# Input and convolution panels first; memory keys and values after them, with the convolution taps beside; memory queries as a pair

## The chip, the cores and the metric

The kernel runs on one core of a Trainium2 chip. TensorE (PE) multiplies matrices and writes PSUM, eight banks of 128x512 fp32; PEld is its weight loader. VectorE (DVE) and ScalarE (ACT) do elementwise work, GpSimd (POOL) a little, and SyncE (SP) issues the DMAs that bring everything in from HBM. Each engine takes its instructions in a fixed order and they wait for each other by semaphores. The metric is the device time of one execution in microseconds (us): 1532.37 us before, the median of three runs (1531.84 to 1532.49).

## The reference

One decoder layer over x (256 tokens, 4096 features), all in fp32, with 256 memory tokens:

```python
proj = x @ w_in[l]                       # 4096 x 11280
(c_a, c_b, c_gate, g_q, g_k, g_v, g_lr, g_gate, m_q, m_gate) = jnp.split(proj, split_idx, axis=-1)
y_conv = _conv_group(c_a, c_b, ...) * jax.nn.silu(c_gate)
y_gla = _gla_group(g_q, g_k, g_v, g_lr, ...) * jax.nn.silu(g_gate)
y_mem = _memory_group(m_q, mem @ w_mem_kv[l]) * jax.nn.silu(m_gate)
mixed = jnp.concatenate([y_conv, y_gla, y_mem], axis=-1)
out = mixed @ w_out[l]
x = _layernorm(DN_ALPHA * x + out, ln_g[l], ln_b[l])
```

The convolution group takes c_a * sigmoid(c_b), 1024 channels, through a causal depthwise convolution of 31 taps, then a layer norm over the channels and a SiLU. The memory group is attention in four heads of m_q against keys and values that come from mem @ w_mem_kv (4096 x 2048).

## The kernel before, in words

**Split products.** Every fp32 operand is split in two, hi (a rounded copy, made by ACT) and lo (the rest, made by DVE): `halves`, lines 104 and 105. A product is three matmuls: hi-hi, hi-lo, lo-hi. So each 128x1024 piece of weights costs ACT one cast, DVE one subtraction and PE twelve matmuls of 512 columns. Pieces of weights have four hi and four lo buffers (`WBUFS`), raw weights three, and the program writes each piece's making three pieces ahead of its use (`AHEAD`).

**Panels and pairs.** A panel (`panel`, line 342) is 512 columns of w_in for all 4096 features: 16 pieces, 192 matmuls. A pair (`pair`, line 411) does two panels at once in 16 chunks of 1 MB. A chunk written "8" has two pieces and 24 matmuls. A chunk written "7" is a Strassen-like one with 21 matmuls: DVE forms two weight combinations from the raw chunk (`tx`, `ty`, lines 466 to 475) and four pieces are split instead of two, one of them half as wide. It also needs sums of x of the same sort (`sums`, line 157). The table `BY7` holds each pair's pattern of 8s and 7s and the units of x that the 7s use.

**Order before.** Seven warm-up matmuls; then the memory keys and values (`mk`, `mv`: 32 steps of two 512 KB halves, line 222), with mem's and x's eight units loaded on the way (`X_AT`); then the panels in the order of `STEPS`: two pairs for the convolution (cb, ca), two single panels of memory queries (mq), two of q, the pair k, five v, the pairs gg, gg and cg, two mg; then the output projection (three pairs, two panels) and the layer norm.

**The convolution.** A pair's outputs leave PSUM in `pair_done` (line 1022); c_a * sigmoid(c_b) is transposed in 32x32 blocks by DVE and put in place by 16 small copies (line 283, half by ACT and half by DVE). Then come 124 taps for each of the two halves of the channels, 248 in all, each one DVE instruction on 128x226 to 128x256 (lines 852 and 861). They are put in the list `fill`, from which a fixed number per piece (`FILLS`) is written beside the matmuls.

**What sets the order.** The order in which instructions are written is not the final one: the build's scheduler (`schedule_with_timeline_sim=True`, line 1424) puts each engine's instructions in an order of its own, within the dependencies.

Of the kernel before, what the change touches and what calls it, by code (L numbers as in the profile page):

```python
# [27 lines left out]
WARM = 7  # L28
EARLY = 5
AHEAD = 3  # L30
X_AT = (9, 12, 15, 18, 21, 24, 27, 30)

C_A, C_B, C_G, G_Q, G_K, G_V, G_LR, G_G, M_Q, M_G = 0, 1024, 2048, 3072, 4096, 5120, 7168, 7184, 9232, 10256


STEPS = (
    [[("cb", i, [(C_B + 512 * i, 512)]), ("ca", i, [(C_A + 512 * i, 512)])] for i in range(2)]
    + [[("mq", i, [(M_Q + 512 * i, 512)])] for i in range(2)]
    + [[("q", i, [(G_Q + 512 * i, 512)])] for i in range(2)]
    + [[("k", i, [(G_K + 512 * i, 512)]) for i in range(2)]]  # L40
    + [[("v", 0, [(G_LR, 16), (G_V, 400)])]]
# [5 lines left out]


BY7 = {
    ("cb", 0): ("8888878787878787", (0, 1, 2), (), (2,)),  # L50
    ("cb", 1): ("8887888788878887", (0, 1), (), (0, 1)),
    ("k", 0): ("8887888788878887", (0, 1), (0, 1), (0, 1)),
    ("gg", 0): ("8888888788878787", (0, 1), (0, 1), ()),
    ("gg", 2): ("8887888788878887", (0, 1), (), (1,)),
    ("cg", 0): ("8888888788888887", (0,), (), (0,)),
}

FILLS = {("cb", 1): 2, ("mq", 0): 2, ("mq", 1): 3, ("q", 0): 2, ("q", 1): 3}


@with_exitstack
def layer_kernel(ctx, tc, xT, memT, xres, w_mem, w_in, w_pairs, w_last, cst, w_gate,
# [116 lines left out]
    def four(ap):  # L179
        return ap.rearrange("p (k t) -> p k t", k=4)  # L180

    x_units = []
    extX = {}
    m_units = []
    mem_banks = [acc.tile([P, 512], F32, tag="acc", name=f"mk_{i}") for i in range(4)] + [
        bank("mv") for _ in range(4)
    ]

    idle = nc.const_aps.tensor(1.0, [P, 512], BF16)
    for _ in range(WARM):  # L190
        nc.tensor.matmul(mem_banks[7], lhsT=idle[:, 0:P], rhs=idle, start=True, stop=True)
    for kt in range(KT):
        if kt == 0:
            mt0 = unit_tiles("mem")
            m_units.append(load(mt0, four(memT[0]), 0, 1))
        elif kt % 4 == 0:
            m_units.append(load_unit("mem", four(memT[kt // 4])))
        mh, ml = m_units[kt // 4]
        raw = w_raw([P, 2, 1024], "wm")
        for half in range(2):  # L200
            if kt:
                nc.sync.dma_start(
                    out=raw[:, half, :], in_=w_mem[kt][:, 1024 * half : 1024 * half + 1024]
                )
            wt = (raw[:, half, :], *w_tiles([P, 1024], "wm"))
            step = 256 if kt == 0 and half == 0 else 512
            if kt == 0:
                for a in range(0, 1024, step):
                    hi, lo = load(wt, w_mem[kt][:, 1024 * half : 1024 * half + 1024], a, a + step)
                if half == 1:  # L210
                    load(mt0, four(memT[0]), 1, 2)
            else:
                hi, lo = wt[1:]
                halves(*wt)
                if kt == 1 and half == 0:
                    load(mt0, four(memT[0]), 2, 4)
                    give(mt0[0])
            for w, stats in ((hi, (mh, ml)), (lo, (mh,))):
                for a in range(0, 1024, step):
                    for mt in range(2):  # L220
                        for s in stats:
                            nc.tensor.matmul(  # L222
                                mem_banks[half * 4 + a // 512 * 2 + mt][:, a % 512 : a % 512 + step],
                                lhsT=s[:, kt % 4, mt * P : (mt + 1) * P],
                                rhs=w[:, a : a + step],
                                start=kt == 0 and w is hi and s is mh and a % 512 == 0,
                                stop=kt == KT - 1 and w is lo,
                            )
        if kt % 4 == 3:
            give(mh, ml)  # L230
            if kt == 3:
                consts = make_consts(nc, cpool, cst, norm_g)
        if kt in X_AT:
            x_units.append(load_unit("x", four(xT[len(x_units)])))
            if len(x_units) <= 3:
                extX[len(x_units) - 1] = sums(*x_units[-1])
# [11 lines left out]
    mk = [unit([P, 2, 512], F32, "mk") for _ in range(2)]  # L248
    mvh = [unit([P, 2, 512], F32R, "mvh") for _ in range(2)]
    mvl = [unit([P, 2, 512], F32R, "mvl") for _ in range(2)]  # L250
    for nb in range(2):
        for mt in range(2):
            evac(mem_banks[nb * 2 + mt], mk[nb][:, mt, :], mt)
    for nb in range(2):
        for mt in range(2):
            halves(mem_banks[4 + nb * 2 + mt], mvh[nb][:, mt, :], mvl[nb][:, mt, :])

    def queue_transpose(src, dst, then, back=False):  # L260


        st = {}

        def blocks():
            t = tmp.tile([P, 1024], F32, tag="T", name=f"T_{serial[0]}", bufs=1)
            serial[0] += 1
            nc.vector.transpose(out=t, in_=src.rearrange("p a b -> p (a b)"))
            give(src)
            st["t"] = t  # L270
# [34 lines left out]
        queue_transpose(src, scratch, go)  # L305

    mkT = {}
    for i in range(2):
        queue_halves(mk[i], lambda hi, lo, i=i: mkT.update({i: (hi, lo)}))

    def products(ps, terms):

# [98 lines left out]
    def pair(chunks, order, stat, ext, then, soon=KT // 2, fills=0, units=False):  # L411


        banks = {}
# [13 lines left out]
        def summed(j):  # L428
# [2 lines left out]
        a11, a21, a12, a22 = (plain(k, tt) for k in range(2) for tt in range(2))  # L431

        eight = (
            ("b", ((1, a21, "N"), (0, a22, "N"), (1, a11, "3"), (0, a12, "3"))),
            ("a", ((0, a21, "4"), (1, a22, "4"), (0, a11, "2"), (1, a12, "2"))),
        )
        seven = (
# [15 lines left out]
        def make(n, i):  # L453
            c, by7, tiles = plan[n]
            if i == 0:
                raw = w_raw([P, 4, 512], "w")
                nc.sync.dma_start(out=raw, in_=chunks[c].rearrange("p (k n) -> p k n", k=4))
                src = st[n] = dict(a=raw[:, 0:2, :], b=raw[:, 2:4, :], c=raw[:, 2:3, :])
                if by7:
                    serial[0] += 1  # L460
# [27 lines left out]
        def use(n, i):  # L488
# [533 lines left out]
    def pair_done(step, b):  # L1022
# [28 lines left out]

        later.extend((one, two, three, four))

    off = 0
    for step in STEPS:
        width = sum(n for _, _, ranges in step for _, n in ranges)
        size = KT * P * width
        flat = w_in[off : off + size]
# [12 lines left out]
        else:  # L1071
            pattern, by7, fresh, _ = BY7[key]

            def queue_sums(fresh=fresh):
# [10 lines left out]
                soon=6 if key == ("gg", 0) else KT // 2,  # L1085
                fills=fills,
                units=True,
            )

    def give_x():  # L1090
        for hi, lo in x_units:
            give(hi, lo)
        assert not fill

# [252 lines left out]
def make_consts(nc, cpool, cst, norm_g):  # L1347
    ident = cpool.tile([P, P], F32, tag="ident", name="ident")
    make_identity(nc, ident)
    negh = cpool.tile([P, 2], F32, tag="negh", name="negh")  # L1350
    nc.gpsimd.memset(negh, -0.5)
    resetm = cpool.tile([P, 256], F32, tag="resetm", name="resetm")
    nc.gpsimd.memset(resetm, 1.0)
    nc.gpsimd.memset(resetm[:, 0:256:64], 0.0)
    cst_sb = cpool.tile([P, 264], F32, tag="cst", name="cst_sb")
    nc.sync.dma_start(out=cst_sb, in_=cst)
    ng_sb = cpool.tile([P, 512], F32, tag="ng", name="ng_sb")
    nc.sync.dma_start(out=ng_sb, in_=norm_g.partition_broadcast(P))
    return ident, negh, resetm, cst_sb, ng_sb


def lay_out(inputs):
# [73 lines left out]
```

## Time and profile before

| | |
|---|---|
| median of three runs | 1532.37 us |
| the profiled execution | 1533.42 us, span 1531.4 us |
| PE busy | 98%, 6857 matmuls |
| DVE busy | 79% |
| ACT busy | 53% |
| mean granted TensorE clock | 0.994 |

Busy is time in which an engine has an instruction under way; instructions overlap a little at their ends, so the distance from one start to the next is what an instruction costs in a row of them. The profile's 40 slices of 38 us show DVE at nine tenths and more from the eighth to the sixteenth (268 to 613 us), from the second convolution pair's start to past the last tap.

### The profile page before, as it was taken

How to read it: one execution, taken by the hardware profiler on the slowest of the kernel's cores; microseconds unless marked ns; L12 is line 12 of the kernel's file. 1: busy time of each engine (PE TensorE's matmuls, PEld its weight loads, DVE VectorE, ACT ScalarE, POOL GpSimd, SP SyncE). 2: the span in 40 equal slices, each digit the busy share in tenths (PEclk: the TensorE clock that was granted, in tenths of full speed). 3: DMA queues.
4: the chain of work that ended last, by engine and by line, in shares of the span. 5: the costliest groups of instructions: out<-in, count | busy, mean ns of one | idle time of the engine just before them, and what ended most of it. 6: DMA issues, size and time to landing. Idle time of an engine off the chain costs nothing.

```text
span 1531.4 us, 18461 instructions
## 1 busy us (share of the span) xinstructions
PE 1507.0 (98%) x6857; PEld 1271.2 (83%) x6857; DVE 1211.7 (79%) x1567; ACT 819.0 (53%) x1005; POOL 48.0 (3%) x59
## 2 busy tenths in 40 slices
PE   8999999999999999999999999999999999999997
PEld 6888888877888878999999888888888887888885
DVE  7755588999999999867475579796777589898955
ACT  6544565544565556656464456574665454545441
POOL 0000000000000000003030000000000000000001
PEclk9999999999999999999999999999999999999998
DMA  9865546545555546554545555555567645555652
GB/s 352 289 207 195 195 174 220 192 165 196 190 178 180 191 155 232 189 198 159 175 164 183 192 192 190 221 192 205 191 235 258 218 167 212 214 206 208 224 220 110
DMA packets 53650, 307.53 MB, mean 201 GB/s; under 512 B 6004, under 2 KB 6900, under 8 KB 26936
## 3 DMA queue, kind: packets, MB, share of 16 engines
q1 hardware_dynamic: 53560, 306.36, 56.5%
q8 instruction: 53, 0.87, 0.2%
q14 instruction: 37, 0.30, 0.1%
HBM read 302.14 MB, written 4.19 MB: 200 GB/s over the span
## 4 chain that ended last, share of the span: by engine, by line
PE 91%; DVE 5%; DMA 2%; issue 1%; ACT 1%; SPq 0%; POOL 0%; DVEq 0%; ACTq 0%
PE acc L355 34%; PE acc L503 30%; PE acc_N L503 8%; PE sm L503 6%; PE mk L222 5%; PE mv L222 5%; DVE low L105 2%; DVE cacc L861 1%; DMA rawwm<-w_mem 1%; PE o L316 1%; DMA ng_sb<-norm_g 1%; PE A L773 1%; PE sc L316 0%; ACT hiw L104 0%; PE mo L316 0%
## 5 line engine op out<-in xcount | busy, mean ns | idle before, releaser
L104 ACT CAST hiw<-raww 128x1024 fp32r<-128x1024 f32 (+2 forms) x496 | 485.6, 991 | 412.7 <-PE acc L355 203.7
L105 DVE TENSOR_TENSOR low<-raww,hiw 128x1024 fp32r<-128x1024 f32 (+2 forms) x496 | 569.2, 1159 | 146.1 <-ACT hiw L104 128.9
L355 PE MATMUL acc<-hiw,hx 128*128 128x512 f32 (+2 forms) x704 | 261.6, 372 | 1.7 <-ACT ca L1032 1.7
L355 PE MATMUL acc<-hiw,lx 128*128 128x512 f32 (+2 forms) x704 | 261.5, 371 | 0.0
L503 PE MATMUL acc<-hiw,hx 128*128 128x512 f32 x480 | 187.3, 390 | 3.9 <-ACT hiw L104 3.8
L503 PE MATMUL acc<-hiw,lx 128*128 128x512 f32 x480 | 186.9, 389 | 0.0
L355 PE MATMUL acc<-low,hx 128*128 128x512 f32 (+2 forms) x704 | 176.2, 371 | 0.0
L355 PEld LDWEIGHTS acc<-hiw,hx 128*128 128x128 f32 x704 | 132.2, 188 | 17.7 <-ACT ca L1032 2.1
L355 PEld LDWEIGHTS acc<-hiw,lx 128*128 128x128 f32 x704 | 132.2, 188 | 15.4
L355 PEld LDWEIGHTS acc<-low,hx 128*128 128x128 f32 x704 | 130.8, 188 | 15.1
L503 PE MATMUL acc<-low,hx 128*128 128x512 f32 x480 | 140.3, 389 | 0.0
L105 DVE TENSOR_TENSOR lowm<-rawwm,hiwm 128x1024 fp32r<-128x1024 f32 (+2 forms) x68 | 78.7, 1161 | 60.6 <-ACT hiwm L104 60.1
L503 PEld LDWEIGHTS acc<-hiw,hx 128*128 128x128 f32 x480 | 90.1, 188 | 24.4 <-ACT hiw L104 5.9
L104 ACT CAST hiwm<-rawwm 128x1024 fp32r<-128x1024 f32 (+2 forms) x68 | 67.7, 1003 | 76.3 <-PE mk L222 35.7
L503 PEld LDWEIGHTS acc<-low,hx 128*128 128x128 f32 x480 | 90.1, 188 | 18.7
L503 PEld LDWEIGHTS acc<-hiw,lx 128*128 128x128 f32 x480 | 90.1, 188 | 18.5
L104 ACT CAST hiw<-ty 128x1024 fp32r<-128x1024 f32 x40 | 42.0, 1050 | 115.7 <-DVE ty L475 70.0
L861 DVE SCALAR_TENSOR_TENSOR cacc<-hT,cst_sb,cacc 128x245 f32<-128x245 f32 (+29 forms) x240 | 99.7, 459 | 0.3
L503 PE MATMUL acc<-hiw,xh 128*128 128x512 f32 x224 | 87.4, 390 | 1.5 <-ACT hiw L104 1.5
L503 PE MATMUL acc<-hiw,xl 128*128 128x512 f32 x224 | 87.1, 389 | 0.0
L105 DVE TENSOR_TENSOR low<-ty,hiw 128x1024 fp32r<-128x1024 f32 x40 | 48.9, 1223 | 37.5 <-ACT hiw L104 27.9
L503 PE MATMUL acc<-low,xh 128*128 128x512 f32 x224 | 66.7, 389 | 0.0
(270 smaller groups left out, 2314.4 us busy)
## 6 DMA issues: line engine op xcount, KB each, us to landing
raww<-w_in SPq DMA_DIRECT2D x144, 1024.0 KB
raww<-w_pairs SPq DMA_DIRECT2D x48, 1024.0 KB
rawwm<-w_mem SPq DMA_DIRECT2D x62, 512.0 KB
raww<-w_in SPq DMA_DIRECT2D x32, 824.0 KB
raww<-w_last SPq DMA_DIRECT2D x16, 1024.0 KB
raww<-w_in SPq DMA_DIRECT2D x8, 832.0 KB
rawx<-xT SPq DMA_DIRECT2D x8, 512.0 KB
xr<-xres SPq DMA_DIRECT2D x8, 512.0 KB
```

Of the source, the lines that this page charges most:

```text
L104: nc.scalar.copy(out=hi, in_=src)
L105: nc.vector.tensor_tensor(out=lo, in0=src, in1=hi.bitcast(F32), op=ALU.subtract)
L222: nc.tensor.matmul(mem_banks[half * 4 + a // 512 * 2 + mt][:, a % 512 : a % 512 + step], lhsT=s[:, kt % 4, mt * P : (mt + 1) * P], rhs=w[: ...
L316: nc.tensor.matmul(ps, lhsT=a, rhs=b, start=t == 0 and k == 0, stop=t == n - 1 and k == 2)
L355: nc.tensor.matmul(banks[tt][:, :width], lhsT=s[:, kt % 4, tt * P : (tt + 1) * P], rhs=w[:, k, :], start=kt == 0 and not second and s is s ...
L503: nc.tensor.matmul(bank_of(bk), lhsT=s, rhs=w[second][:, slot, :], start=first[bk] == (n, nm, j) and not second and s is sh, stop=last[bk] ...
L773: nc.tensor.matmul(ps[:, at : at + n], lhsT=keys[:, j, k0 : k0 + P], rhs=qs[:, j, q0 : q0 + n], start=dk == 0, stop=dk == 1,)
L861: nc.vector.scalar_tensor_tensor(out=a, in0=h, scalar=dw_sb[:, cb, j : j + 1], in1=a, op0=ALU.mult, op1=ALU.add)
```

## The change

The order of stages becomes: the two convolution pairs, with x loaded on the way; then memory keys and values as pieces of the same stream, with five taps written beside each half step (`MEM_FILLS`); then the memory queries as a pair (three matmuls fewer in each of its four 7s); the rest as before. The 7s of the first pairs use other units of x. The copies that follow a block transpose are all ACT's. The constants' loads move to the third chunk. The first chunk of the first pair is loaded in parts, between parts of x.

```diff
-X_AT = (9, 12, 15, 18, 21, 24, 27, 30)
+X_AT = {0: (1,), 1: (2,), 3: (3,), 4: (6,), 5: (4,), 6: (7,), 7: (5,)}
...
-    + [[("mq", i, [(M_Q + 512 * i, 512)])] for i in range(2)]
+    + [[("mq", i, [(M_Q + 512 * i, 512)]) for i in range(2)]]
...
-    ("cb", 0): ("8888878787878787", (0, 1, 2), (), (2,)),
-    ("cb", 1): ("8887888788878887", (0, 1), (), (0, 1)),
...
+    ("cb", 0): ("8888888887878787", (6, 7), (), ()),
+    ("cb", 1): ("8888878787878787", (5, 6, 7), (5,), (5,)),
+    ("mq", 0): ("8888888887878787", (6, 7), (), (6, 7)),
...
-FILLS = {("cb", 1): 2, ("mq", 0): 2, ("mq", 1): 3, ("q", 0): 2, ("q", 1): 3}
+FILLS = {("cb", 1): 1}
+MEM_FILLS = 5
...
-                f = nc.scalar.copy if a % 2 else nc.vector.tensor_copy
-                f(
+                nc.scalar.copy(
...
+                if beside and n == 0:
+
+                    x0 = unit_tiles("x")
+                    hi, lo = w_tiles([P, 2, 512], "w")
+                    for k in range(2):
+                        load(x0, four(xT[0]), k, k + 1)
+                        load((raw[:, 2:4, :], hi, lo), ap[:, 2:4, :], 1 - k, 2 - k)
+                    st[n, "b"] = hi, lo
+                    nc.sync.dma_start(out=raw[:, 0:2, :], in_=ap[:, 0:2, :])
+                    x_units[0] = load(x0, four(xT[0]), 2, 4)
+                    give(x0[0])
+                else:
+                    nc.sync.dma_start(out=raw, in_=ap)
+                if beside:
+                    beside(n)
...
-            for _ in range(min(fills, len(fill))):
-                fill.popleft()()
             if i == len(tiles) - 1:
+                for _ in range(min(fills, len(fill))):
+                    fill.popleft()()
...
+        def use(kt, half):
+            while later and half == 1:
+                later.popleft()()
...
+            mh, ml = m_units[kt // 4]
+            hi, lo = tiles.pop((kt, half))
+            for w, parts in ((hi, (mh, ml)), (lo, (mh,))):
+                for a in range(2):
+                    for mt in range(2):
+                        for s in parts:
+                            nc.tensor.matmul(
+                                banks[half * 4 + a * 2 + mt],
...
+            do_work(-(-len(work) // max(1, KT - kt)))
+            for _ in range(min(MEM_FILLS, len(fill))):
+                fill.popleft()()
...
+        for kt in range(KT):
+            for half in range(2):
+                push(lambda kt=kt, half=half: make(kt, half), lambda kt=kt, half=half: use(kt, half))
+        after(done)
...
     for step in STEPS:
+        if step[0][:2] == ("mq", 0):
+            memory()
```

DVE in the second convolution pair, around a 7, before; `low` is the lo of a piece, `tx` and `ty` are a 7's combinations, `cacc` is a tap's accumulator, and x2 stands for two such rows in a row:

```order
L861 SCALAR_TENSOR_TENSOR cacc_2231<-hT_2210,cst_sb,cacc_2231 128x254 x2
L105 TENSOR_TENSOR low_2345<-raww_2337,hiw_2344 128x512
L472 TENSOR_TENSOR ty_2340<-raww_2337,tx_2339 128x512
L861 SCALAR_TENSOR_TENSOR cacc_2231<-hT_2210,cst_sb,cacc_2231 128x254
L105 TENSOR_TENSOR low_2363<-raww_2337,hiw_2362 128x1024
L861 SCALAR_TENSOR_TENSOR cacc_2231<-hT_2210,cst_sb,cacc_2231 128x254
L861 SCALAR_TENSOR_TENSOR cacc_2231<-hT_2210,cst_sb,cacc_2231 128x253 x2
L475 TENSOR_TENSOR ty_2340<-raww_2337,ty_2340 128x512
```

The same engine and pair now (the lines' numbers are those of the changed file: 108 for 105, 424 to 433 for 466 to 475, 821 for 861):

```order
L424 TENSOR_TENSOR tx_1050<-raww_1048 128x1024
L821 SCALAR_TENSOR_TENSOR cacc_1020<-hT_928,cst_sb,cacc_1020 128x253
L108 TENSOR_TENSOR low_1013<-tx_951,hiw_1012 128x1024
L108 TENSOR_TENSOR low_1027<-raww_1024,hiw_1026 128x1024
L821 SCALAR_TENSOR_TENSOR cacc_1020<-hT_928,cst_sb,cacc_1020 128x252 x3
L108 TENSOR_TENSOR low_1038<-raww_1024,hiw_1037 128x1024
L430 TENSOR_TENSOR ty_1051<-raww_1048,tx_1050 128x512
L821 SCALAR_TENSOR_TENSOR cacc_1020<-hT_928,cst_sb,cacc_1020 128x252
L108 TENSOR_TENSOR low_1056<-raww_1048,hiw_1055 128x512
L821 SCALAR_TENSOR_TENSOR cacc_1020<-hT_928,cst_sb,cacc_1020 128x251 x3
L108 TENSOR_TENSOR low_1069<-raww_1048,hiw_1068 128x1024
L433 TENSOR_TENSOR ty_1051<-raww_1048,ty_1051 128x512
```

The scheduler has put taps among the pieces of this pair as before, 82 from the first tap to the pair's last piece where there were 77; the pair now has six 7s where there were four. From that first tap to the last piece the order holds 35 instructions on 128x1024 and 17 on 128x512 beside the taps; before, 27 and 9.

DVE in the middle of the memory keys and values, before (`lowm` is the lo of a memory weight piece, `lx` of a unit of x):

```order
L105 TENSOR_TENSOR lowm_1048<-rawwm_1045,hiwm_1047 128x1024
L105 TENSOR_TENSOR lowm_1065<-rawwm_1045,hiwm_1064 128x1024
L105 TENSOR_TENSOR lowm_1089<-rawwm_1086,hiwm_1088 128x1024
L105 TENSOR_TENSOR lowm_1106<-rawwm_1086,hiwm_1105 128x1024
L105 TENSOR_TENSOR lowm_1130<-rawwm_1127,hiwm_1129 128x1024
L105 TENSOR_TENSOR lx_1351<-rawx_1349,hx_1350 128x1024
```

and now:

```order
L108 TENSOR_TENSOR lowm_2189<-rawwm_2160,hiwm_2188 128x1024
L821 SCALAR_TENSOR_TENSOR cacc_1672<-hT_1565,cst_sb,cacc_1672 128x248 x3
L821 SCALAR_TENSOR_TENSOR cacc_1672<-hT_1565,cst_sb,cacc_1672 128x247
L108 TENSOR_TENSOR lowm_2215<-rawwm_2212,hiwm_2214 128x1024
L821 SCALAR_TENSOR_TENSOR cacc_1672<-hT_1565,cst_sb,cacc_1672 128x247 x3
L108 TENSOR_TENSOR lowm_2237<-rawwm_2212,hiwm_2236 128x1024
L821 SCALAR_TENSOR_TENSOR cacc_1672<-hT_1565,cst_sb,cacc_1672 128x246 x3
L108 TENSOR_TENSOR lowm_2260<-rawwm_2257,hiwm_2259 128x1024
```

Three or four taps stand between two pieces here, where there was none.

SP's DMA queue at the start, before (`rawmem`, `rawwm`: memory tokens and their weights; `rawx`: a unit of x):

```order
L131 DMA rawmem_97<-memT 128x256
L131 DMA rawwm_103<-w_mem 128x256 x4
L131 DMA rawwm_103<-w_mem 128x512 x2
L131 DMA rawmem_97<-memT 128x256
L202 DMA rawwm_165<-w_mem 128x1024
L131 DMA rawmem_97<-memT 128x512
```

and now, as far as the fourth chunk (`raww_202`):

```order
L409 DMA raww_102<-w_in 128x1024
L134 DMA rawx_103<-xT 128x512
L134 DMA rawx_124<-xT 128x1024
L413 DMA raww_134<-w_in 128x2048
L134 DMA rawx_136<-xT 128x1024
L413 DMA raww_164<-w_in 128x2048
L1401 DMA cst_sb<-cst 128x264
L1402 DMA ng_sb<-norm_g 128x512
L134 DMA rawx_204<-xT 128x1024
L134 DMA rawx_244<-xT 128x1024
L134 DMA rawx_295<-xT 128x1024
L134 DMA rawx_335<-xT 128x1024
```

Ahead of these rows stand two quarters of the first unit of x (128x256) and the first chunk's second half in two parts (128x512). The second chunk (`raww_134`) waits for 2.1 MB, and four units of x stand between the third chunk and the fourth.

## Rows read from the trace of the kernel before

**Rows 1.** The page: busy time of the engines; the chain's shares by engine
```profile
PE 1507.0 (98%) x6857; PEld 1271.2 (83%) x6857; DVE 1211.7 (79%) x1567; ACT 819.0 (53%) x1005; POOL 48.0 (3%) x59
...
PE 91%; DVE 5%; DMA 2%; issue 1%; ACT 1%; SPq 0%; POOL 0%; DVEq 0%; ACTq 0%
```

**Rows 2.** Timeline of PE late in the second convolution pair: start, us, engine, line, operation
```profile
329.76 0.39 PE L503 MATMUL acc<-low,hx 128*128 128x512 f32 x1
329.99 0.39 PE L503 MATMUL sm<-low,hx 128*128 128x512 f32 x1
332.58 0.50 PE L503 MATMUL acc<-hiw,hx 128*128 128x512 f32 x1 [2.21 <-ACT hiw L104]
...
333.22 0.63 PE L503 MATMUL sm<-hiw,eh 128*128 128x512 f32 x1
333.64 0.63 PE L503 MATMUL sm<-hiw,el 128*128 128x512 f32 x1
```

**Rows 3.** Windows: stretch, length, busy and count by engine, clock, DMA share, GB/s
```profile
0.00:40.00 40.00, 34.27 (x142) 26.11 (x143) 28.52 (x33) 27.04 (x31) 1.68 (x14) 0.96 0.93 354
40.00:186.00 146.00, 146.00 (x646) 120.90 (x645) 84.21 (x78) 65.92 (x65) 0.00 (x0) 1.00 0.65 221
186.00:270.00 84.00, 84.00 (x373) 69.54 (x372) 72.99 (x87) 53.87 (x70) 0.00 (x0) 1.00 0.54 192
270.00:361.00 91.00, 85.94 (x368) 69.37 (x366) 89.33 (x147) 44.77 (x53) 0.00 (x0) 0.98 0.55 185
330.00:340.00 10.00, 7.79 (x28) 5.97 (x27) 10.00 (x18) 6.94 (x7) 0.00 (x0) 0.83 0.31 105
```

**Rows 4.** Timeline of DVE: a 7's halves and pieces, then taps between pieces
```profile
205.74 0.68 DVE L472 TENSOR_TENSOR ty<-raww,tx 128x512 f32<-128x512 f32 x1
206.34 0.68 DVE L105 TENSOR_TENSOR low<-raww,hiw 128x512 fp32r<-128x512 f32 x1
...
309.97 1.22 DVE L105 TENSOR_TENSOR low<-ty,hiw 128x1024 fp32r<-128x1024 f32 x1
311.11 1.25 DVE L861 SCALAR_TENSOR_TENSOR cacc<-hT,cst_sb,cacc 128x251 f32<-128x251 f32 x3
312.28 1.21 DVE L105 TENSOR_TENSOR low<-tx,hiw 128x1024 fp32r<-128x1024 f32 x1
```

**Rows 5.** Tile cacc: durations, first and last start of the first taps
```profile
L852 DVE TENSOR_SCALAR cacc<-hT,cst_sb x8: 402/408/409, 294.9 to 406.2; 128x256 f32<-128x256 f32 x8
```

**Rows 6.** Timeline of DVE: the last piece of the second pair
```profile
359.32 1.22 DVE L105 TENSOR_TENSOR low<-tx,hiw 128x1024 fp32r<-128x1024 f32 x1
```

**Rows 7.** The page's groups: count, busy us and mean ns, idle before and releaser
```profile
L104 ACT CAST hiw<-ty 128x1024 fp32r<-128x1024 f32 x40 | 42.0, 1050 | 115.7 <-DVE ty L475 70.0
```

**Rows 8.** Line 283, copies after a transpose: durations, first and last start
```profile
L283 DVE COPY S<-T x112: 270/284/289, 188.0 to 1182.8; 32x256 f32<-32x256 f32 x112
L283 ACT COPY S<-T x112: 401/403/410, 188.6 to 1183.8; 32x256 f32<-32x256 f32 x112
```

**Rows 9.** Timeline of ACT: the eight copies of the first conv transpose
```profile
289.46 3.32 ACT L283 COPY hT<-T 32x256 f32<-32x256 f32 x8
```

**Rows 10.** Timeline of PE: the longest wait of the start
```profile
32.28 0.50 PE L222 MATMUL mk<-hiwm,hmem 128*128 128x512 f32 x1 [3.17 <-ACT hiwm L104]
```

**Rows 11.** Windows of the start, and of the pair k
```profile
0.00:4.00 4.00, 3.15 (x7) 0.90 (x7) 0.42 (x1) 2.03 (x3) 1.68 (x14) 1.00 0.39 115
4.00:8.00 4.00, 3.88 (x26) 3.84 (x27) 2.34 (x5) 1.90 (x5) 0.00 (x0) 1.00 0.79 221
8.00:12.00 4.00, 2.88 (x12) 1.68 (x10) 1.18 (x3) 1.66 (x3) 0.00 (x0) 1.00 0.92 343
12.00:40.00 28.00, 24.37 (x99) 19.69 (x100) 24.58 (x25) 21.46 (x22) 0.00 (x0) 0.94 1.03 408
564.00:572.00 8.00, 7.20 (x30) 4.99 (x29) 7.85 (x12) 4.12 (x5) 0.00 (x0) 1.00 0.35 127
```

More of the change, by code (lines that the diff above doesn't have):

```diff
@@ L49 @@
 BY7 = {
-    ("cb", 0): ("8888878787878787", (0, 1, 2), (), (2,)),
-    ("cb", 1): ("8887888788878887", (0, 1), (), (0, 1)),
[L52 to L55, printed above, removed]
-}
-FILLS = {("cb", 1): 2, ("mq", 0): 2, ("mq", 1): 3, ("q", 0): 2, ("q", 1): 3}
+    ("cb", 0): ("8888888887878787", (6, 7), (), ()),
+    ("cb", 1): ("8888878787878787", (5, 6, 7), (5,), (5,)),
+    ("mq", 0): ("8888888887878787", (6, 7), (), (6, 7)),
+    ("k", 0): ("8887888788878887", (6, 7), (6, 7), (6, 7)),
+    ("gg", 0): ("8888888788878787", (6, 7), (6, 7), ()),
+    ("gg", 2): ("8887888788878887", (6, 7), (), (7,)),
+    ("cg", 0): ("8888888788888887", (6,), (), (6,)),
+}
+FILLS = {("cb", 1): 1}
+MEM_FILLS = 5
 @with_exitstack
@@ L180, in four @@
         return ap.rearrange("p (k t) -> p k t", k=4)
-    x_units = []
+    x_units = {}
     extX = {}
[L184 to L187, printed above, removed]
     idle = nc.const_aps.tensor(1.0, [P, 512], BF16)
+    warm = bank("warm")
     for _ in range(WARM):
[L191 to L236, printed above, removed]
@@ L237, in layer_kernel @@
+        nc.tensor.matmul(warm, lhsT=idle[:, 0:P], rhs=idle, start=True, stop=True)
+    consts, load_consts = make_consts(nc, cpool, cst, norm_g)
     ident, negh, resetm, cst_sb, ng_sb = consts
@@ L246, in evac @@
             nc.vector.tensor_copy(out=dst, in_=ps)
[L248 to L256, printed above, removed]
     def queue_transpose(src, dst, then, back=False):
@@ L307, in layer_kernel @@
     mkT = {}
-    for i in range(2):
-        queue_halves(mk[i], lambda hi, lo, i=i: mkT.update({i: (hi, lo)}))
     def products(ps, terms):
@@ L409, in in_order, with pair @@
         return [(p7.pop(0), True) if ch == "7" else (p8.pop(0), False) for ch in pattern]
-    def pair(chunks, order, stat, ext, then, soon=KT // 2, fills=0, units=False):
+    def pair(chunks, order, stat, ext, then, soon=KT // 2, fills=0, units=False, beside=None):
         banks = {}
@@ L433, in pair @@
         eight = (
-            ("b", ((1, a21, "N"), (0, a22, "N"), (1, a11, "3"), (0, a12, "3"))),
+            ("b", ((1, a21, "N"), (1, a11, "3"), (0, a22, "N"), (0, a12, "3"))),
             ("a", ((0, a21, "4"), (1, a22, "4"), (0, a11, "2"), (1, a12, "2"))),
@@ L456, in make @@
                 raw = w_raw([P, 4, 512], "w")
-                nc.sync.dma_start(out=raw, in_=chunks[c].rearrange("p (k n) -> p k n", k=4))
+                ap = chunks[c].rearrange("p (k n) -> p k n", k=4)
+                if beside and n == 0:
[12 more added lines that the diff above has]
+                    beside(n)
                 src = st[n] = dict(a=raw[:, 0:2, :], b=raw[:, 2:4, :], c=raw[:, 2:3, :])
@@ L479, in make @@
             nm = tiles[i][0]
+            if (n, nm) in st:
+                return
             w = tuple(t[:, : 1 if nm == "c" else 2, :] for t in w_tiles([P, 2, 512], "w"))
@@ L1052, in pair_done, with memory, make, done @@
         later.extend((one, two, three, four))
+    mk, mvh, mvl = [], [], []
+    def memory():
+        m_units, raws, tiles, banks = [], {}, {}, []
+        def make(kt, half):
+            if half == 0:
+                if kt == 0:
+                    m_units.append(load_unit("mem", four(memT[0])))
+                raws[kt] = w_raw([P, 2, 1024], "wm")
+            raw = raws[kt][:, half, :]
+            nc.sync.dma_start(out=raw, in_=w_mem[kt][:, 1024 * half : 1024 * half + 1024])
+            if half == 1 and kt % 4 == 1 and kt < KT - 4:
+                m_units.append(load_unit("mem", four(memT[kt // 4 + 1])))
+            tiles[kt, half] = w_tiles([P, 1024], "wm")
+            halves(raw, *tiles[kt, half])
+        def use(kt, half):
+            while later and half == 1:
+                later.popleft()()
+            if kt == 0:
+                for i in range(4):
+                    serial[0] += 1
+                    pool, tag = (sm, "sm") if half else (acc, "acc")
+                    banks.append(
+                        pool.tile([P, 512], F32, tag=tag, name=f"m{'kv'[half]}_{serial[0]}")
+                    )
+            mh, ml = m_units[kt // 4]
[6 more added lines that the diff above has]
+                                banks[half * 4 + a * 2 + mt],
+                                lhsT=s[:, kt % 4, mt * P : (mt + 1) * P],
+                                rhs=w[:, 512 * a : 512 * a + 512],
+                                start=kt == 0 and w is hi and s is mh,
+                                stop=kt == KT - 1 and w is lo,
+                            )
+            if half and kt % 4 == 3:
+                give(mh, ml)
+            if later:
+                later.popleft()()
+            do_work(-(-len(work) // max(1, KT - kt)))
+            for _ in range(min(MEM_FILLS, len(fill))):
+                fill.popleft()()
+        def done():
+            mk.extend(unit([P, 2, 512], F32, "mk") for _ in range(2))
+            mvh.extend(unit([P, 2, 512], F32R, "mvh") for _ in range(2))
+            mvl.extend(unit([P, 2, 512], F32R, "mvl") for _ in range(2))
+            for nb in range(2):
+                for mt in range(2):
+                    evac(banks[nb * 2 + mt], mk[nb][:, mt, :], mt)
+            for nb in range(2):
+                for mt in range(2):
+                    halves(banks[4 + nb * 2 + mt], mvh[nb][:, mt, :], mvl[nb][:, mt, :])
+            for i in range(2):
+                queue_halves(mk[i], lambda hi, lo, i=i: mkT.update({i: (hi, lo)}))
+        for kt in range(KT):
+            for half in range(2):
+                push(lambda kt=kt, half=half: make(kt, half), lambda kt=kt, half=half: use(kt, half))
+        after(done)
@@ L1054, in layer_kernel, with load_x, beside @@
+    def load_x(u):
+        x_units[u] = load_unit("x", four(xT[u]))
+        if u >= 6:
+            work.append(lambda: extX.update({u: sums(*x_units[u])}))
+    def beside(n):
+        for u in X_AT.get(n, ()):
+            load_x(u)
+        if n == 2:
+            load_consts()
     off = 0
     for step in STEPS:
+        if step[0][:2] == ("mq", 0):
+            memory()
         width = sum(n for _, _, ranges in step for _, n in ranges)
@@ L1087, in layer_kernel @@
                 units=True,
+                beside=beside if off == size else None,
             )
     def give_x():
-        for hi, lo in x_units:
+        for hi, lo in x_units.values():
             give(hi, lo)
@@ L1355, in make_consts, with load @@
     cst_sb = cpool.tile([P, 264], F32, tag="cst", name="cst_sb")
-    nc.sync.dma_start(out=cst_sb, in_=cst)
     ng_sb = cpool.tile([P, 512], F32, tag="ng", name="ng_sb")
-    nc.sync.dma_start(out=ng_sb, in_=norm_g.partition_broadcast(P))
-    return ident, negh, resetm, cst_sb, ng_sb
+    def load():
+        nc.sync.dma_start(out=cst_sb, in_=cst)
+        nc.sync.dma_start(out=ng_sb, in_=norm_g.partition_broadcast(P))
+    return (ident, negh, resetm, cst_sb, ng_sb), load
 def lay_out(inputs):
```

## Prediction

> **What bounds the kernel now.** The page comes first: PE is busy 98% of the span and holds 91% of the chain that ended last [rows 1], so a change counts by the matmuls it removes and by the time in which PE has none to run. The windows give both. From 40 to 186, the memory keys and values, 646 matmuls start in 146 us: 0.226 us each, the spacing that the timeline also shows (329.76 to 329.99) [rows 2, 3]. This is the price of a 512-wide matmul below. From 186 to 270, the first convolution pair, 373 at that spacing fill the window. From 270 to 361, the second pair, 368 make 83.2 us of 91: 7.8 us are lost [rows 3]. From 0 to 40 there are 7 warm-ups, 24 half-wide matmuls and 111 whole ones: 24 x 0.113 + 111 x 0.226 = 27.8 us, so 12.2 are lost, the start's latency and a wait of 3.17 us among them [rows 3, 10].
>
> Who makes PE wait in the second pair? The timeline shows PE waiting 2.21 us for ACT's cast [rows 2]. The page's group shows for whom ACT waits: casts of `ty` waited 70 us in all for DVE [rows 7]. DVE is busy 89.3 of the 91 us [rows 3]. Starts on DVE are the real prices: a 128x1024 instruction takes 1.14 us (309.97 to 311.11), three taps 1.17, so 0.39 each, a 128x512 one 0.60 [rows 4]. From the pair's first tap at 294.9 [rows 5] the order holds 77 taps, 27 whole and 9 half instructions: 77 x 0.39 + 27 x 1.14 + 9 x 0.60 = 66.2 us, hence 361.1; the trace ends the last piece at 359.32 + 1.14 = 360.5 [rows 6]. So DVE ran without a pause and set the pace. PE began this pair at about 186.3 + 366 x 0.226 = 269.0 and needed 372 x 0.226 = 84.1 us, to 353.1; DVE came 7.4 us later, the loss of the window within half a microsecond.
>
> **The change, part by part.** *Matmuls.* The memory queries as a pair lose 4 x 3 = 12; the memory's first half step swaps 24 half-wide ones for 12 whole ones. Both pairs together hold as many as before (6 + 4 sevens become 4 + 6). Net 24 x 0.113 = 2.7 us less. PE has no spare time there, so the gain is whole: **-2.7**.
>
> *The second pair.* It now needs 366 x 0.226 = 82.7 us of PE. DVE's first tap waits for the transposed product. The eighth piece's lo stands before the transpose and needs the buffer of the fourth, free after 4 x 12 x 0.226 = 10.8 us; the lo and the transpose, taken as 1.14 each, bring 13.1. Then ACT alone makes 16 copies; eight took 3.32 us [rows 9], so 6.6 for 16, and with half a microsecond for a cast in front the first tap starts about 20.3 us into the pair (25.9 before). From there the order holds 82 taps, 35 whole and 17 half instructions: 32.0 + 39.9 + 10.2 = 82.1 us. The last piece is ready at 102.4, 19.7 late. PE's order puts eight memory matmuls, 1.8 us, before the last two lo pieces, which leaves 17.9. The taps are written beside the memory stage, but the scheduler has moved them up into this pair, and two more 7s stand here, each with 6.3 us of DVE (1.14 for `tx`, twice 0.60 for `ty`, 0.60 and three times 1.14 for the pieces) against 21 x 0.226 = 4.7 of PE.
>
> The memory stage does not win this back: PE's lost time stays lost. There DVE has a piece (1.14) and three or four taps (2.3 to 2.7 us together) per 2.71 us of PE, and at its start the leftovers of the pair too, so for some pieces it stays level; I add 0.5. The loss is 18.4 against 7.8: **+10.6**. The bounds: with copies that cost nothing the first tap comes at 13.7 and the loss is 11.8 (+4); with a first tap as late as before, 25.9, it is 24.0 (+16). The low clock after a long wait (0.83 in the window of 330 to 340, matmuls 0.42 us apart, the level of 1.2 GHz [rows 2, 3]) adds nothing while DVE sets the pace.
>
> *The start.* By 12 us the DMAs had moved 4 x (115 + 221 + 343) = 2.7 MB, then 408 GB/s [rows 11]. Now the second chunk is complete at 3.15 MB (two chunks, two units of x), 13.1 us by those rates; with a cast of 1.05 [rows 7], 14.1. Only the first chunk's 5.4 us are done by then: 8.7 lost. The next two chunks last until 25.0. The fourth chunk stands behind the constants and four units, at 8.3 MB: 25.7 + 1.05 = 26.8, another 1.8. That is 10.5 against 12.2: **-1.7**. From there a chunk arrives in 2.6 us and is used in 5.4. The bounds: 8 if the larger parts land sooner, 15 if PE runs its first two chunks at the low clock too.
>
> *The pair k.* From 564 to 572 it starts 30 matmuls, 6.8 us of 8, with DVE busy 7.85 [rows 11]. The taps that ran until then are done by the memory stage now: **-1.2**, between 0 and -1.2.
>
> *The copies.* ACT's take 0.40, DVE's 0.28 [rows 8]. Moving 176 of them frees DVE where it binds (counted above) and gives ACT blocks of 6.6 us. A piece of an 8 lasts 2.71 us on PE and four hi buffers cover 10.8, so the block hides there; among a 7's short pieces less so: **+0.5**, 0 to +6.
>
> *The memory stage itself* has 146 us of PE and 84 of DVE busy [rows 3]; the rest of the taps, 163 x 0.39 = 64 us, fits. Its first weights are asked for during the pair before, so the 3.17 us wait for them [rows 10] belongs to the start that goes.
>
> Sum: -2.7 + 10.6 - 1.7 - 1.2 + 0.5 = +5.5. The profiled execution took 1533.4 us, 1.0 above the median of the runs shown, so 1538.9 there and **1537.9** for the median. The likeliest case's own range is 1533 to 1545.
>
> **The rivals.** *The taps really run beside the memory stage, and PE hides DVE's delay by taking hi parts of later pieces first.* For it: PE's order interleaves hi and lo, and DVE has 62 us to spare in the memory window [rows 3]. Against it: the same freedom did not save the 7.8 us before, and the order fixes 82 taps in the pair. Then the second pair loses no more than before and the sum is -2.7 - 1.7 - 1.2 = -5.6: 1526.8. If its 7.8 us went too, 1519. It decides if the second pair loses less than 12 us. The Trainium skill ("Perfetto Trace Analysis", Optimization Strategy) says that where the most-contended engine changes over time, interleaving those regimes may help. By that rule this rival would hold; the mean of DVE over both stages is indeed under PE's, but the rows above are of a stage in which DVE alone binds.
>
> *The start gets longer.* Matmuls after a wait ran 0.42 us apart instead of 0.23 [rows 2]. The new start has three waits in its first 27 us. If the second chunk begins at the low clock, and the first loads come no faster than before, 15 us are lost there: +4.5 on the forecast, 1542.4.
>
> *ACT's blocks of copies.* Among 7s, pieces of 1.36 us with four buffers cover 5.4 us, less than 6.6 plus the casts. Four of the 22 transposes falling among 7s would cost 1.5 us each: 1543.9. Against it: ACT is half idle [rows 1].
>
> *The terms cancel.* If the first tap comes when its operands allow, without the copies' block, the pair's loss is 12 to 13 and the sum near zero: 1532.4.
>
> **How the numbers follow.** The forecast 0.50, faster by interleaving 0.14, a longer start 0.13, ACT's blocks 0.09, cancelled 0.14. About 0.2% (3 us) can be told from no change. Faster: the first rival and a sliver, 0.15. Within 0.2%: the last one and the low edge of the forecast, 0.19. Slower: 0.66. The range 1528 to 1546 takes in the last three rivals and the cancelled case, and leaves out most of the interleaving one and the sum of two bad ends.
>
> **What would show it.** In the changed profile the window of the second pair should show DVE without pauses, PE some 18 us short of its matmuls, and waits of 2 to 5 us at each 7, released by ACT's cast of `ty` or DVE's lo; in the memory queries no loss; from 0 to 40 a loss near 10; in the pair k none. It is wrong if the second pair loses under 12 us, if waits stand in the memory stage after its first ten pieces, or if blocks of copies release PE.

## The result and the profile after

The changed kernel takes 1542.52 us (median of four runs, 1542.0 to 1542.82) against 1532.43 us in the same runs: 10.1 us slower, a ratio of 1.0066 with a 95% interval of 1.0054 to 1.0078. The forecast was 1537.9, 5.5 us slower. The profiled execution took 1542.59 us, its span 1540.8. One execution of the last experiment's kernel, 1770.6 us at a granted clock of 0.807, is left out of that kernel's median below.

The page of the changed kernel: busy time of the engines, then the chain's shares by engine, to be held against [rows 1].

```profile
PE 1509.8 (98%) x6833; PEld 1270.8 (82%) x6833; DVE 1180.4 (77%) x1414; ACT 889.4 (58%) x1187; POOL 48.0 (3%) x59
...
PE 85%; DVE 7%; ACT 3%; issue 3%; DMA 2%; POOL 0%; SPq 0%; DVEq 0%; ACTq 0%
```

PE has 24 matmuls fewer and DVE 31 us less to do, and yet the chain that ended last goes more often through DVE and ACT. The windows of the changed kernel say where: the start, the rest of the first pair, the second pair, the memory keys and values, the memory queries (columns as in [rows 3]).

```profile
0.00:40.00 40.00, 35.10 (x137) 26.43 (x138) 30.43 (x35) 24.42 (x27) 1.69 (x14) 1.00 0.85 325
40.00:97.00 57.00, 55.51 (x245) 45.67 (x244) 46.05 (x50) 31.98 (x35) 0.00 (x0) 1.00 0.57 203
97.00:204.00 107.00, 95.59 (x382) 74.57 (x382) 103.92 (x164) 56.68 (x71) 0.00 (x0) 0.94 0.51 173
204.00:375.00 171.00, 170.78 (x754) 141.13 (x753) 161.66 (x262) 95.97 (x126) 1.97 (x2) 1.00 0.66 220
375.00:455.00 80.00, 80.00 (x355) 66.26 (x354) 56.09 (x56) 51.88 (x75) 0.00 (x0) 1.00 0.57 195
```

The loss of a window is its length less 0.2265 us for each matmul, the distance between two 512-wide ones when none waits. In the second pair 382 matmuls make 86.5 of 107 us: 20.5 are lost, where the pair of before lost 7.8 [rows 3]. The start loses 40 - 130 x 0.2265 = 10.6 (seven of its 137 are warm-ups; 12.2 before), the first pair 1.5, the memory stage 0.2, the queries nothing.

The first pair's loss is one wait, of 1.49 us, which ends at 64.27. PE waits for the lo of a 7's `ty`. On DVE this lo stands behind the `tx` of the next 7, and that `tx` waited for its chunk of weights to land:

```profile
61.86 1.22 DVE L424 TENSOR_TENSOR tx<-raww 128x1024 f32<-128x1024 f32 x1 [5.20 <-DMA raww<-w_in]
```

The second pair on the timelines of ACT and DVE: the copies ahead of the first tap; the last piece. Between them, the tile of the taps and, for the window of the pair, who waited longest for whom (us, times, longest).

```profile
111.13 6.63 ACT L228 COPY hT<-T 32x256 f32<-32x256 f32 x16 [0.31 <-DVE T L214]
```

```profile
L812 DVE TENSOR_SCALAR cacc<-hT,cst_sb x8: 395/402/412, 117.8 to 241.1; 128x256 f32<-128x256 f32 x8
```

```profile
ACT hiw L107 <- DVE ty L433: 21.9, 5, 6.9
```

```profile
198.00 1.21 DVE L108 TENSOR_TENSOR low<-tx,hiw 128x1024 fp32r<-128x1024 f32 x1
```

From the first tap at 117.8 to the last piece at 198.0 DVE has no pause, as it had none from 294.9 to 359.3 before [rows 5, 6], and ACT waits for `ty` five times. The end of the pair on PE:

```profile
194.89 0.80 PE L463 MATMUL acc<-hiw,hx 128*128 128x512 f32 x1 [2.52 <-ACT hiw L107]
...
199.33 0.63 PE L1049 MATMUL mk<-hiwm,hmem 128*128 128x512 f32 x1
199.75 0.63 PE L1049 MATMUL mk<-hiwm,lmem 128*128 128x512 f32 x1
...
201.28 0.39 PE L463 MATMUL acc<-low,hx 128*128 128x512 f32 x1
```

Of the sixteen matmuls between this wait and the last lo twelve come 0.42 us apart, the level of 1.2 GHz, and so PE reaches the last lo at 201.28, though it was ready at 198.00 + 1.14 = 199.1.

### The profile page after: what moved, and what is told of

Read it like the earlier page. It is cut to its first block, busy times and chain, and to the rows that moved or that the text cites. A ratio compares the mean times of both kernels' runs of the same rounds, so it can differ in the third digit from the quotient of the medians.

```text
span 1540.8 us, 18445 instructions
## 1 busy us (share of the span) xinstructions
PE 1509.8 (98%) x6833; PEld 1270.8 (82%) x6833; DVE 1180.4 (77%) x1414; ACT 889.4 (58%) x1187; POOL 48.0 (3%) x59
## 4 chain that ended last, share of the span: by engine, by line
PE 85%; DVE 7%; ACT 3%; issue 3%; DMA 2%; POOL 0%; SPq 0%; DVEq 0%; ACTq 0%
PE acc L463 31%; PE acc L298 25%; PE acc_N L463 9%; PE sm L463 7%; PE mv L1049 6%; PE mk L1049 5%; DVE low L108 2%; ACT S L228 2%; DVE cacc L821 2%; DMA rawx<-xT 1%; DMA raww<-w_in 1%; ACT hiw L107 1%; PE A L733 1%; PE o L259 1%; PE mo L259 0%
## 5 line engine op out<-in xcount | busy, mean ns | idle before, releaser
L108 DVE TENSOR_TENSOR low<-raww,hiw 128x1024 fp32r<-128x1024 f32 (+3 forms) x497 | 565.4, 1153 | 194.2 <-ACT hiw L107 170.6
L107 ACT CAST hiw<-raww 128x1024 fp32r<-128x1024 f32 (+3 forms) x497 | 480.8, 985 | 340.8 <-PE acc L463 150.1
L298 PE MATMUL acc<-hiw,hx 128*128 128x512 f32 (+2 forms) x576 | 211.8, 368 | 0.3 <-ACT hiw L107 0.3
L298 PE MATMUL acc<-hiw,lx 128*128 128x512 f32 (+2 forms) x576 | 211.7, 368 | 0.0
L463 PE MATMUL acc<-low,hx 128*128 128x512 f32 x560 | 177.1, 390 | 5.8 <-DVE low L108 5.8
L298 PE MATMUL acc<-low,hx 128*128 128x512 f32 (+2 forms) x576 | 141.7, 366 | 0.0
L298 PEld LDWEIGHTS acc<-low,hx 128*128 128x128 f32 x576 | 107.2, 188 | 10.5
L107 ACT CAST hiw<-ty 128x1024 fp32r<-128x1024 f32 x44 | 46.2, 1050 | 120.3 <-DVE ty L433 82.1
L107 ACT CAST hiwm<-rawwm 128x1024 fp32r<-128x1024 f32 x64 | 66.4, 1052 | 72.1 <-PE mv L1049 27.0
L821 DVE SCALAR_TENSOR_TENSOR cacc<-hT,cst_sb,cacc 128x255 f32<-128x255 f32 (+29 forms) x240 | 98.9, 460 | 0.0
L228 ACT COPY S<-T 32x256 f32<-32x256 f32 x224 | 90.4, 403 | 8.9 <-DVE T L214 3.6
L108 DVE TENSOR_TENSOR lowm<-rawwm,hiwm 128x1024 fp32r<-128x1024 f32 x64 | 77.5, 1216 | 2.7 <-ACT hiwm L107 2.3
```

What stands on the lines that cost most here:

```text
L107: nc.scalar.copy(out=hi, in_=src)
L108: nc.vector.tensor_tensor(out=lo, in0=src, in1=hi.bitcast(F32), op=ALU.subtract)
L228: nc.scalar.copy(out=to[32 * b : 32 * b + 32, :, :, a, :], in_=frm[32 * a : 32 * a + 32, :, :, b, :],)
L298: nc.tensor.matmul(banks[tt][:, :width], lhsT=s[:, kt % 4, tt * P : (tt + 1) * P], rhs=w[:, k, :], start=kt == 0 and not second and s is s ...
L463: nc.tensor.matmul(bank_of(bk), lhsT=s, rhs=w[second][:, slot, :], start=first[bk] == (n, nm, j) and not second and s is sh, stop=last[bk] ...
L821: nc.vector.scalar_tensor_tensor(out=a, in0=h, scalar=dw_sb[:, cb, j : j + 1], in1=a, op0=ALU.mult, op1=ALU.add)
```

## The experiments

Nine kernels were run, each timed in five rounds beside the kernel before. The theory: DVE, loaded with taps among the pair's 7s, sets the second pair's pace. Its rivals: the 7s' own chain of `tx`, `ty`, cast and lo; ACT's blocks of copies; a loss that only moves. The expectations put the changed kernel's loss in the pair at 21.2 us; the window above gives 20.5. The medians of the kernel before were 1531.78 us in the first four runs, 1532.77 in the next three and 1533.13 in the last two; each ratio is taken to its own.

**The taps held back.** The taps read a copy of their weights which DVE makes from a memory piece, so they cannot start earlier:

```diff
-FILLS = {("cb", 1): 1}
-MEM_FILLS = 5
+FILLS = {("cb", 1): 0, ("mq", 0): 3}
+MEM_FILLS = 4
...
+            dw = dw_sb if s < 6 else dw2
...
+    def open_taps(hi):
+        nc.vector.scalar_tensor_tensor(
+            out=taps_sb,
+            in0=hi[:, 0:248].bitcast(F32),
+            scalar=0.0,
+            in1=cst_sb[:, 0:248],
+            op0=ALU.mult,
+            op1=ALU.add,
+        )
```

`dw2` is a view of the copy, `taps_sb`.

> The changed kernel, with the taps from the seventh shift on held back until the first memory piece is cast (they read a copy of the tap weights that is made from that piece), and four taps written beside each memory half step. In the second pair DVE's order then holds 24 taps from the first tap to the last piece instead of 82, by the durations of the trace 58.8 us of work instead of 81.6. Theory (DVE's own work sets the second pair's pace, and the taps are what is too much): with the first tap 21.0 us into the pair again, the last piece is ready at 79.8, before PE's 82.7 are over; the pair's loss falls from 21.2 to under 3. In the memory stage DVE has 157 us of work from the first to the 61st piece against 163 of PE, so it loses 2 at the most. Time 1542.5 - 18 = about 1524 (1522 to 1527). Rival one (the chains of the six 7s, tx, ty, cast, lo, make PE wait whatever stands between them): the pair still loses over 10, 1532 or more. Rival two (the work only moves, the memory stage loses what the pair gains): about 1540.

Measured: 1535.83 us, ratio 1.0027 (1.0016 to 1.0038); about 7 us less than the changed kernel, not 18. Two windows of it, the second pair and a stretch of the memory queries:

```profile
98.00:190.00 92.00, 89.32 (x381) 73.08 (x380) 82.70 (x105) 56.80 (x71) 0.00 (x0) 0.96 0.60 202
...
418.00:430.00 12.00, 6.41 (x28) 4.97 (x27) 9.70 (x13) 4.47 (x7) 0.00 (x0) 0.83 0.22 71
```

The pair loses 92 - 86.3 = 5.7 instead of 20.5, so the taps were most of it. The timeline of DVE has the 24 that are left between 118.5 and 139.1, among the first two 7s, and PE's longest waits there are 1.66 and 1.02 us. But the queries lose 12 - 6.3 = 5.7 which they did not lose before. Their timelines:

```profile
419.05 2.74 DVE L870 SCALAR_TENSOR_TENSOR y<-y,cmv,cgam 128x512 f32<-128x512 f32 x4 [2.98 <-DMA cgam<-conv_g]
```

```profile
423.62 2.62 ACT L876 ACTIVATE y<-y 128x512 f32<-128x512 f32 x4 [5.40 <-DVE y L873]
```

```profile
429.37 0.80 PE L465 MATMUL acc<-hiw,hx 128*128 128x512 f32 x1 [5.59 <-ACT hiw L107]
```

The taps ended later, and with them the convolution's layer norm, which now stood in front of a 7's casts on ACT and waited for its own rows to load. Neither rival gave this; the later runs that hold taps back also move that norm.

**Four 7s in the second pair.**

```diff
-    ("cb", 1): ("8888878787878787", (5, 6, 7), (5,), (5,)),
+    ("cb", 1): ("8888878788878887", (6, 7), (), ()),
```

> The changed kernel with four 7s instead of six in the second pair, spread over the second half of it, and no third unit of sums. Theory (DVE's count sets the pace): from the first tap to the last piece the order holds 87 taps, 32 whole and 11 half instructions, 76.5 us instead of 81.6, while PE needs 84.0 instead of 82.7. The loss falls by 5.1 + 1.4 to about 14.7, six matmuls of a 7 more cost 1.4: 1542.5 - 5.1 = 1537.4 (1535 to 1540). Rival (only the taps matter, and there are five more of them): no change or slower, 1542.5 to 1544.

Measured: 1533.10 us, ratio 1.0010 (1.0002 to 1.0019), 9.4 less instead of 5.1. The window of the pair:

```profile
95.00:196.00 101.00, 94.14 (x391) 75.66 (x391) 97.67 (x158) 53.63 (x67) 0.00 (x0) 0.95 0.54 184
```

The pair loses 12.4, two less than counted, and the first pair nothing, where it had lost 1.5: 244 matmuls start in the 55 us ahead of this window. The edit also takes away the sums of a third unit of x, which stood on DVE and ACT in the first pair: in the four kernels run here with two units that window loses nothing, in the five with three, the changed one among them, 0.5 to 4.0 us by the execution. In the five, the `tx` shown above starts at 60.1 to 62.5 us, when its chunk has landed; in the four, at 57.1 to 57.6. So the two 7s more also cost the first pair something; how their sums delay that chunk was not shown.

**The copies shared again.**

```diff
-                nc.scalar.copy(
+                f = nc.scalar.copy if a % 2 else nc.vector.tensor_copy
+                f(
```

> The changed kernel with the 16 copies after a transpose shared between ACT and DVE again, as before the change. Theory: the copies of the first conv transpose take 3.3 us instead of 6.6, so the first tap comes 3.3 us earlier; from it to the last piece the order holds 78 taps and 79.0 us instead of 81.6, so the last piece of the second pair comes 5.9 us earlier and the pair loses 15.3 instead of 21.2. The wait of PE after a block of 16 copies at 966.9 (1.1 us) goes as well. Time 1542.5 - 7 = 1535.5 (1533 to 1538). Rival (the copies lie beside other work, and DVE now has to pay 88 of them): 1541 to 1544.

Measured: 1537.04 us, ratio 1.0037 (1.0026 to 1.0049), 5.5 less. The window of the pair:

```profile
99.00:202.00 103.00, 92.52 (x381) 73.67 (x381) 102.42 (x164) 52.95 (x62) 0.00 (x0) 0.95 0.52 179
```

It loses 103 - 86.3 = 16.7 instead of 20.5, 3.8 us less where 5.9 were forecast. Later waits go too. The changed kernel's timelines of ACT and PE show one:

```profile
959.12 6.64 ACT L228 COPY S<-T 32x256 f32<-32x256 f32 x16 [1.22 <-DVE xl L108]
```

```profile
966.89 0.50 PE L463 MATMUL acc<-hiw,hx 128*128 128x512 f32 x1 [0.98 <-ACT hiw L107]
```

With the copies shared there is no wait over 0.3 us between 220 and 1290. The time came out 1.5 us above the theory and inside its range.

**The memory queries as two panels again.** One line of `STEPS` is put back; in `BY7` the second pair now also gives back the sums of the two units that the queries no longer use.

> The changed kernel with the memory queries as two single panels again. Theory: 12 more matmuls at 0.2265 us, nothing hidden since PE has no spare time there: 1542.5 + 2.7 = 1545.2 (1544 to 1546.5). Rival (the pair's 7s cost DVE and the handing over as much as they save): 1542.5 or below.

Measured: 1544.68 us, ratio 1.0083 (1.0070 to 1.0096): 2.2 slower than the changed kernel, so the pair is worth its twelve matmuls and the rival falls.

**No tap in the second pair, six 7s.** As the first experiment, but no tap is free to come early, `FILLS` has 4 in place of 3, and there is a second copy of the weights made at the 29th memory piece for the second half's taps; and:

```diff
-            if i == 1:
-                queue_conv_norm()
...
+        if key == ("k", 0):
+            after(queue_conv_norm)
```

> The changed kernel with all taps held back until the memory stage (the first half's until the first memory piece is cast, the second half's until the 29th), four written beside each half step, and the end of the convolution's layer norm moved to the pair k. The second pair keeps its six 7s and has no tap at all; DVE's order has 43 us of pieces, combinations and transposes from about 21 us into the pair, PE 62. Theory (taps among the 7s are what PE waits for, the remaining 7.9 us of the first experiment too, since its 24 taps all stood among the first two 7s): the pair loses under 2 instead of 21.2. In the memory stage the order gives DVE 164 us from the first to the 61st piece against 163 of PE, its first six steps 21 against 16, so PE loses 5 to 8 there. Time 1542.5 - 19 + 7 = about 1530 (1527 to 1533). Rival (a 7's own chain of tx, ty, cast and lo makes PE wait): the pair still loses 6 to 8, 1536 or more.

Measured: 1527.65 us, ratio 0.9967 (0.9954 to 0.9979). The second pair, then the memory stage:

```profile
96.00:180.00 84.00, 84.00 (x372) 69.58 (x371) 71.65 (x78) 55.44 (x70) 0.00 (x0) 1.00 0.63 219
180.00:346.00 166.00, 163.44 (x718) 133.86 (x717) 161.54 (x277) 82.13 (x100) 0.00 (x0) 1.00 0.64 208
```

372 matmuls fill the 84 us: with the same six 7s, and the copies still all ACT's, the pair loses nothing. This decides between the taps on one side and the 7s' own chain and ACT's blocks on the other. The memory stage loses 166 - 162.6 = 3.4, where 5 to 8 were forecast. The rival of a loss that only moves holds in part: counted matmul by matmul, this kernel is 22.3 us ahead of the changed one at the pair's end, 19.0 at the end of the memory stage, 18.5 behind the queries and 14.4 at 997 us of the changed trace.

**Four 7s and shared copies together.**

> The changed kernel with both smaller edits: four 7s in the second pair and the copies shared between ACT and DVE. Theory (both work through the time at which DVE has the pair's last pieces ready): with four 7s alone the pair lost 12.8; the first tap now comes 3.3 us earlier and the order holds 74.5 us from it to the last piece instead of 76.5, so 4 to 5 us less, and the waits behind blocks of 16 copies later (1.1 and 0.5 us) go: 1533.1 - 6 = 1527 (1525 to 1530). Rival (the two save the same wait): 1532 to 1534.

Measured: 1528.11 us, ratio 0.9970 (0.9959 to 0.9982): the two add up. From 96 to 192 us PE starts 383 matmuls, so the pair still loses 9.2; the taps are still in it.

**All edits together,** with the first 16 taps free to come in the second pair.

> The changed kernel with four 7s, shared copies, and the taps held back as in the run without taps in the pair, but for the first 16, and the convolution's layer norm ended at the pair k. From the first tap to the last piece DVE's order holds 49.3 us where PE has 63; in the memory stage 156.5 from the first to the 61st piece against 163 of PE (18 against 16 in the first six); 49 taps are left for the memory queries. Theory: the pair loses 2 at the most, the memory stage 2: 1533.1 (four 7s alone) - 11 + 2 - 1.5 (blocks of copies) = about 1522.5 (1520 to 1526), faster than before the change. Rival (taps left over for the memory queries wait for units and stop the stream there, as the layer norm did in the first experiment): 1528 to 1531.

Measured: 1525.14 us, ratio 0.9947 (0.9934 to 0.9961). The second pair, then a stretch of the queries:

```profile
97.00:182.00 85.00, 85.00 (x376) 70.38 (x375) 72.53 (x92) 49.86 (x59) 0.00 (x0) 1.00 0.63 218
...
410.00:425.00 15.00, 12.48 (x47) 9.52 (x47) 13.68 (x22) 8.76 (x13) 0.00 (x0) 0.89 0.40 140
```

Pair and memory stage lose nothing (760 matmuls start in the 172 us between). The queries lose 15 - 10.6 = 4.4 at their first 7s, and DVE's timeline has seven taps behind the first `tx` there. The theory had no such loss, but up to 4 us for pair and memory stage, and missed by 2.6. The rival had the place right and the price too high.

**Thirty-two taps free instead of 16.**

> As the run of all edits together, with the first 32 taps free to come in the second pair instead of 16. That run lost 4.7 us of PE at the first 7s of the memory queries, where taps were left over. Now DVE's order has 55.5 us from the first tap to the pair's last piece (49.3 with 16 taps), PE 63; 33 taps instead of 49 are left after the memory stage, none after the first 7 of the memory queries begins. Theory: the 4.7 us go, the pair loses 2 at the most: 1525.1 - 4.7 + 1 = about 1521.5 (1520 to 1524). Rival (the 16 taps more stand among the pair's 7s and cost there what they saved): 1525 to 1528.

Measured: 1522.63 us, ratio 0.9934 (0.9921 to 0.9946), the fastest of all. The pair, and the queries:

```profile
97.00:182.00 85.00, 83.64 (x369) 68.93 (x368) 76.87 (x104) 48.28 (x57) 0.00 (x0) 1.00 0.63 216
...
354.00:440.00 86.00, 86.00 (x381) 71.24 (x380) 78.42 (x112) 54.26 (x75) 0.00 (x0) 1.00 0.57 195
```

The pair pays 1.4 for the taps, the queries nothing, which bears out that the taps left over were what the queries waited for.

**The kernel before with its taps held back,** to see whether the order of stages matters at all.

> The kernel before, its order of stages unchanged, with the taps from the seventh shift on held back until the first piece of the first single panel of memory queries, four written per piece from there. The second pair's order keeps 24 taps of 77. Theory (the stages behind the second pair had no room left on DVE, so only memory keys and values placed after the pairs give the taps room): the pair's loss of 8 goes, but by the order DVE needs 288 us from the first tap to the 104th piece after it, where it needed 276, and the taps end among pieces of the later panels in one block of over 50 us per eight pieces: 1532.4 - 8 + 12 = about 1536 (1532 to 1545). Rival (holding the taps back is all that was needed, with or without the change): 1524 to 1527.

Measured: 1555.77 us, the median of five, ratio 1.0151 (1.0136 to 1.0165): slower by more than the theory gave (1532 to 1545). The rival falls, at least for taps written four per piece. What costs the other 20 us is not known.

## Why the prediction came out as it did

The direction, the place and the cause were right, and the time lies in the range. The time is 4.6 us above the forecast: one term was too small by 2.1, one was put at nothing, one was 1.3 too small, and two hits within 0.1 us are in part luck.

*Matmuls, -2.7.* The page counts 24 fewer. Twelve are those of the queries' 7s, the whole of the 2.7 us; the other twelve come from 24 half-wide ones that became 12 whole ones, which saves no time. The prediction's 24 x 0.113 is the same number as 12 x 0.226. Taking the twelve back cost 2.2 us.

*The second pair, +10.6.* It was 20.5 - 7.8 = +12.7. DVE's last piece was forecast for 102.4 us into the pair and ready at 102.3: 199.1, counted from 96.8, where this pair would begin with all 372 matmuls of the first behind it. This hit is in part luck. The first tap came 117.8 - 96.8 = 21.0 us into the pair instead of 20.3, and from there the order took 81.3 us instead of 82.1. What failed is the sentence that the low clock adds nothing while DVE sets the pace. It adds nothing to a wait that follows. But the last wait ended with work in hand, eight matmuls of the pair and the eight of the memory stage that the forecast used to fill DVE's delay. Twelve of these sixteen ran at 1.2 GHz, so PE came 2.1 us late to a lo that was ready. That is the miss of this term to within half a microsecond.

*The start, -1.7.* 10.6 lost against 12.2: -1.6. By 13.45 us, when the second chunk's first matmul starts, 8.0 were lost (8.7 forecast), and the fourth chunk cost 2.4 (1.8). The other eight kernels begin with the same order, and this window lost 9.9 to 12.1 in them, so a hit within 0.1 is luck.

*The first pair, forecast at nothing.* It lost 1.5, the wait behind a chunk of weights that landed late. The prediction did not follow the sums of the third unit, which the two 7s more need, into the stage that now makes them; the kernels without them lose nothing there.

*Copies, +0.5.* The later waits behind blocks of 16 took about 1.8 us by the trace of the run with shared copies; the rival that gave them 6 was too dear.

*The pair k, -1.2.* No wait over 0.3 us stands there now (between 530 and 960 in the changed trace). The parts make -2.7 + 12.7 - 1.6 + 1.5 + 1.8 - 1.2 = 10.5, against 9.4 between the two spans; the 1.1 between them was not traced.

*The rivals.* Interleaving was to decide below 12 us of loss in the second pair; it was 20.5. The terms did not cancel, the start was not longer. The first rival, though, was right on what the order of stages allows. With the taps kept out of the pair by a dependency and the layer norm ended later, the same order of stages runs at 1527.65 us. With four 7s, shared copies and 32 free taps besides, it runs at 1522.63. The Trainium skill ("Perfetto Trace Analysis", Optimization Strategy) says that interleaving stages may help where the most-contended engine changes over time. Those two runs agree, as the pair's loss fell from 7.8 us before to nothing and to 1.4; the change as it stands does not, as its taps were moved back into the pair.

*The signs.* DVE ran without a pause and PE was 20.5 us short (18 forecast), but PE's single waits in the pair were 0.2 to 2.5 us, not 2 to 5. One sign of being wrong did show, in small: at 966.89 PE waited 0.98 us for a cast that stood behind a block of copies.

## What to carry to other kernels

Where a scheduler is free to reorder, work that is written beside a roomy stage need not run there: here 82 taps went into the stage before. Read the final order, and count the engine's microseconds per piece in it, before believing that work was moved. What held the taps in their stage here was something to read that is made there. A count of one engine's instructions from the first tap to the last piece came within 0.8 us of the 81.3 measured. When a wait ends, look at the spacing of the matmuls that follow before pricing them: here it was 0.42 us after some waits and 0.23 after others.

## What was not expected of the hardware

The granted clock was 0.94 over the pair that waited and 1.00 over the one that did not (experiment without taps). In the changed kernel 25 matmuls of the second pair and the memory stage's start stood 0.42 us apart instead of 0.2265, together 5.0 us, half of it after the last wait. The low clock did not follow every wait: after one of 2.27 us, at 26.90, matmuls stood 0.23 us apart. After one of 2.17, at 166.65, which followed another of 1.22 at 163.74, six stood 0.42 apart. The five kernels with three units of sums have the same instructions in the same order on PE, DVE and ACT up to 96 us, and yet the first pair lost 0.5 to 4.0 us in their profiled executions. The same `tx` waited for its chunk in all five, and the chunk landed at 60.1 to 62.5 us; why it landed at different times was not followed up. The runs of one kernel lay up to 5 us apart (1534.96 to 1540.26 with shared copies, 1529.64 to 1534.43 for the kernel before in the same job).
